# Where sixteen output-matrix products and the weights behind them stand among eight attention heads

## The chip, the core and the metric

The kernel runs on one core of a Trainium2 chip. The metric is the device time of one execution in microseconds (us), lower is better. Of the kernel before there are three timed runs: 1076.58, 1077.21 and 1078.67 us, median 1077.21.

The engines of the core are named as in the profile: PE is the matrix engine (TensorE), with PEld for its weight loads; DVE is VectorE, ACT is ScalarE, POOL is GpSimd, and SP issues most of the DMA transfers. Each has a queue of its own and works it off in order; semaphores make one engine wait for another. A line such as L853 is line 853 of the kernel.

## What is computed

One decoder block in float32 on a sequence of 1024 tokens with 1024 features. Eight heads of a softmax attention with a forgetting term and a gated branch ("spatial gating") share an input projection. Their results are put side by side and multiplied by one output matrix:

```python
xn = rmsnorm(h, norm_mix_g)
proj = xn @ w_in
att = forgetting_attention(q, k, v, log_f)            # 8 heads of 64
sg = chunked_spatial_gating(u, vg, gain, w_s, b_s)    # 512 wide
mix = concatenate([att, sg], axis=-1)
h = h + mix @ w_out                                   # (1024, 1024)
h = h + conv_ffn(rmsnorm(h), w_up, conv_w, conv_b, w_down)
return rmsnorm(h)
```

In `forgetting_attention` the logits are `q k^T / 8 + c_i - c_j` for j <= i, where c is a running sum of log-sigmoids. The change concerns `mix @ w_out`, which splits by rows of `w_out`: rows 512 to 1023 meet `sg` (the gated branch), rows 0 to 511 meet `att`.

## The kernel before, in words

**Precision.** A float32 operand is split into a rounded high part and the remainder (low part). One product is then three passes on PE: high by high, high by low, low by high. `split_w` (L150) makes the two parts: a cast on ACT or POOL gives the high part, a subtraction on DVE or POOL the low part.

**Stages.** In order of time: the input projection (to about 200 us), the spatial gating, the attention heads (about 216 to 395 us), the output matrix's attention half with the second norm (to about 445 us), the up projection with convolution, and the down projection. The last two are long runs of 128x512 products.

**An attention head** (`att_head`, L752). Five transfers of SP load the head's queries, keys and forgetting sums into two tiles (`x1`, `x2`, two buffers each, L754 to L760); so the loads of head h+2 start when head h has made its logits. The head goes through four steps i = 0 to 3, each with two blocks of 128 queries. For a block, POOL masks the diagonal (`affine_select`, L776), PE makes the logits (L783, L784), DVE adds and takes the row minimum (L786) and ACT the exponential (L789). Then, by pairs of key blocks, PE transposes (L812), ACT casts the high part (L813), DVE subtracts for the low part (L814) and PE multiplies by V (L822). ACT and DVE bring the sums out of PSUM (L828, L829). `row_tail` (L724) turns the row sums around through DRAM, and `pair_end` (L738) scales a pair of heads and splits it; for the first three pairs that is POOL's work, at step 2 of heads 2, 4 and 6.

**The filler** (`sg_out`, L833). The gated branch's half of `mix @ w_out` is 2 halves of the columns by 8 blocks of 128 tokens: 16 products of 12 matmuls (L851 to L853). It is a generator. The list `FILLS` (L20) says how many products are pulled ahead of the transposes of each of the 32 steps. Before the first product of each half, the half's weights are loaded (`wos`, two transfers of 512 KB into buffers `raw`) and split into four tiles `whl` (ACT casts, POOL subtracts). For each product a block of x is loaded into `raw`, DVE adds the product to it (L854), and SP stores the sum to `hpd` (L855). `raw` and `whl` have four buffers each. The list before gives 1, 2, 1, 2 products to the steps of heads 0 and 1 and 1, 2, 1 to the first three of head 2; the second half's weights are loaded and split at the place of product 8, the second product of head 1's step 1.

**The attention's output weights** (`wo_load`, L862). Four blocks of `woa`, 512 KB each. Blocks 0 and 1 go into the four `whl` tiles as soon as the filler is through with them, blocks 2 and 3 into tiles `G`. All casts and subtractions are POOL's. Blocks 0 and 1 stand behind the masks of head 5, blocks 2 and 3 behind the last mask of head 7; the transfers stand behind those of head 4. The products that need them (`wmm`, L959) begin at the end of head 7.

**Order.** The code is written in the order of importance. A planner puts it into one queue an engine when the kernel is built, from modelled costs: the earliest in the code that is ready goes first. `after(tc, later, earlier)` (L59) binds only the order of two instructions in the plan. So one step's instructions can stand among those of the step before, and an edit can move others around it.

Of the kernel before, what the change touches and what calls it, by code (L numbers as in the profile page):

```python
# [9 lines left out]
F32R = mybir.dt.float32r  # L10
BF16 = mybir.dt.bfloat16
AF = mybir.ActivationFunctionType
ALU = mybir.AluOpType
AX = mybir.AxisListType
P = 128
# [1 line left out]
BIG = 3.0e38  # L17
NFF = 22
WARM = 11
FILLS = [1, 2] * 10 + [2] + [0] * 11  # L20
FCFG = ("b", 4, 4)


# [35 lines left out]
def after(tc, later, earlier):  # L59
    tc.add_manual_dep(later.ins, earlier.ins.name, mybir.DependencyInfo(  # L60
        mybir.DependencyClass.NoSync, mybir.DependencyReason.DATA), reason="order")
# [3 lines left out]
def block_kernel(ctx: ExitStack, tc: tile.TileContext, xT, xtok, wuv, wv, wqk, wf, cpk, bfv,  # L65
                 ggain, g2r, gfr, wsp, woa, wos, wup, wdn, out):
    nc = tc.nc
    act, dve, pool, pe, sp = Line(nc.scalar, tc), Line(nc.vector, tc), Line(nc.gpsimd, tc), nc.tensor, nc.sync
# [6 lines left out]
    drm = ctx.enter_context(tc.tile_pool(name="drm", bufs=1, space=bass.MemoryType.DRAM))  # L75
    FILL = FILLS
    FTAG, FB, BB = FCFG
# [4 lines left out]
    def nm(s):  # L82
        uid[0] += 1
        return f"{s}_{uid[0]}"
# [6 lines left out]
    def sb(tag, shape, dt=F32):  # L91
        return (raws if tag == "raw" else late if tag in LATE else early).tile(shape, dt, tag=tag, bufs=BUFS[tag], name=nm(tag))
# [4 lines left out]
    def fbank():  # L97
        return psa.tile([P, 512], F32, tag=FTAG, bufs=FB, name=nm("pf"))
# [4 lines left out]
    def f32(ap):  # L103
        return ap.bitcast(F32)
# [45 lines left out]
    def split_w(src, hl, hi_eng="act", lo_eng="dve"):  # L150
        h, l = hl
        if hi_eng == "act":
            act.copy(h, src)  # L153
        elif hi_eng == "pool":
            pool.tensor_copy(h, src)
        else:
            dve.tensor_copy(h, src)
        eng = dve if lo_eng == "dve" else pool
        return eng.tensor_tensor(out=l, in0=src, in1=f32(h), op=ALU.subtract)  # L159
# [81 lines left out]
    def tsplit(src, neg=False, gate="keys"):  # L241
        w = ring()
        if neg:
            act.activation(w[:, 0], src, AF.Copy, scale=-1.0)
            behind(dve.scalar_tensor_tensor(out=w[:, 1], in0=src, scalar=-1.0, in1=f32(w[:, 0]),
                                            op0=ALU.mult, op1=ALU.subtract), gate)
        else:
            split_w(src, (w[:, 0], w[:, 1]))
        return w
# [85 lines left out]
    for j in range(2):  # L335
        t1, t2, t3 = tmp[j]
        for c in range(2):
            k = 2 * j + c
# [27 lines left out]
    for j in range(2):  # L366
        t2 = tmp[j][1]
        for c in range(2):
            k = 2 * j + c
# [35 lines left out]
    class Weights:  # L405
# [9 lines left out]
        def split(self, *names):  # L415
            for n in names:
                self.w[n] = tsplit(self.src[n])
# [223 lines left out]
    for hf in (1, 0):  # L641
        for c in range(4):
            src = vgt[hf][:, :, c * P:(c + 1) * P].rearrange("p t (g d) -> p g t d", g=2)
# [75 lines left out]
    loads = [None] * 8  # L719
    exs = []  # L720
    rows = [None] * 8
    sels = [[] for _ in range(8)]
# [29 lines left out]
    def att_head(h, order=(0, 1, 2, 3)):  # L752
# [13 lines left out]
        for i in order:  # L766
# [25 lines left out]
            if h == 7 and i == 3:  # L792
                wo_load((2, 3))
                row_tail(7, None)
# [36 lines left out]
            pair_end(3, None)  # L831

    def sg_out():  # L833
        for hf in range(2):
            o = slice(hf * 512, hf * 512 + 512)
            whs = []
            for kp in range(2):
                wr = sb("raw", [P, 2, 512])
                sp.dma_start(out=wr, in_=wos[hf, kp])
                for j in range(2):  # L840
                    w = sb("whl", [P, 2, 512], F32R)
                    split_w(wr[:, j, :], (w[:, 0], w[:, 1]), "act", "pool")
                    whs.append(w)
            for tt in range(8):
                ts_ = slice(tt * P, (tt + 1) * P)
                hs = sb("raw", [P, 512])
                sp.dma_start(out=hs, in_=xtok[ts_, o])
                ps = fbank()
                for k in range(4):
                    w = whs[k]  # L850
                    pe.matmul(ps, sgT[k][:, 0, ts_], w[:, 0, :], start=(k == 0), stop=False)  # L851
                    pe.matmul(ps, sgT[k][:, 0, ts_], w[:, 1, :], start=False, stop=False)  # L852
                    pe.matmul(ps, sgT[k][:, 1, ts_], w[:, 0, :], start=False, stop=(k == 3))  # L853
                dve.tensor_tensor(out=hs, in0=ps, in1=hs, op=ALU.add)  # L854
                sp.dma_start(out=hpd[tt, :, o], in_=hs)  # L855
                yield

    filler = sg_out()

    wo = []  # L860

    def wo_load(ks):  # L862
        for k in ks:
            wr = sb("raw", [P, 1024])
            after(tc, sp.dma_start(out=wr, in_=woa[k]), loads[4])
            if k < 2:
                w = [sb("whl", [P, 2, 512], F32R) for _ in range(2)]
            else:
                t = sb("G", [P, 2, 1024], F32R)
                w = [t[:, :, hf * 512:hf * 512 + 512] for hf in range(2)]  # L870
            for hf in range(2):
                src = wr[:, hf * 512:hf * 512 + 512]
                after(tc, pool.tensor_copy(w[hf][:, 0], src), sels[5][2 * k + hf] if k < 2 else sels[7][3])
                pool.tensor_tensor(out=w[hf][:, 1], in0=src, in1=f32(w[hf][:, 0]), op=ALU.subtract)
            wo.append(w)

    for h in range(8):
        if h == 7:
            for _ in filler:
                pass  # L880
            wo_load((0, 1))
        att_head(h)
# [569 lines left out]
```

## Time and profile before

| what | us |
|---|---|
| median of three runs | 1077.21 |
| the profiled execution, whole | 1076.71 |
| its span, first to last instruction | 1075.0 |
| PE busy in the span | 1062.7 |
| DVE busy | 892.4 |
| ACT busy | 568.0 |
| POOL busy | 249.5 |
| filler's products on PE, first to last start | 225.0 to 304.3 |
| second half's weights: ACT casts and POOL subtractions | 260.8 to 266.5 |
| first exponential of heads 0 to 7 | 227.0, 254.9, 287.7, 311.5, 324.9, 340.4, 356.6, 370.7 |

The profile is that of one execution; its whole time is 1.7 us over its span and 0.5 us under the median. A matmul's end is modelled, so PE's busy time says little on how full PE is. What counts is when the next matmul starts. The granted clock of PE was 0.998 of full speed over the span.

### The profile page before, as it was taken

Reading aid. Unit: us, or ns where it says so; the run is one execution under the profiler, and the core shown is the slowest. Engines: PE = TensorE matmul, PEld = TensorE weight load, DVE = VectorE, ACT = ScalarE, POOL = GpSimd, SP = SyncE. Lnnn points to the kernel's source line nnn. Section 1 sums busy time; section 2 is a strip of 40 time slices with the busy share of each in tenths; the row PEclk is TensorE's granted clock in tenths of the full one; section 3 lists DMA queues with packets and bytes.
Section 4 is the critical chain, followed back from the end, with each engine's and each line's share of the span. In section 5 each row is a group of like instructions: output and inputs, shape, how many; then the busy total and the mean of one; then the engine's idle time right before and its main releaser. Section 6 shows DMA issues by size and latency. Waiting matters only on the chain.

```text
span 1075.0 us, 14470 instructions
## 1 busy us (share of the span) xinstructions
PE 1062.7 (99%) x5013; PEld 876.6 (82%) x5013; DVE 892.4 (83%) x1363; ACT 568.0 (53%) x984; POOL 249.5 (23%) x223
## 2 busy tenths in 40 slices
PE   9999999999999999999999999999999999999997
PEld 7888788787888888878888888888888888888886
DVE  5985798775689969999899999989988776898774
ACT  6666644554468855764444444444444444454653
POOL 0002134233046541054333333333322000000000
PEclk9999999999999999999999999999999999999999
DMA  9242267937557445132244513222331899433442
GB/s 345 90 140 96 74 156 218 278 118 224 188 166 207 129 137 185 72 117 98 98 137 164 170 69 127 98 98 98 108 118 45 289 326 317 125 95 97 141 125 96
DMA packets 66297, 160.80 MB, mean 150 GB/s; under 512 B 7976, under 2 KB 8240, under 8 KB 66224
## 3 DMA queue, kind: packets, MB, share of 16 engines
q1 hardware_dynamic: 65792, 159.32, 45.4%
q8 instruction: 39, 0.64, 0.2%
q10 hardware_dynamic: 432, 0.57, 0.1%
q14 instruction: 34, 0.28, 0.1%
HBM read 117.06 MB, written 42.80 MB: 149 GB/s over the span
## 4 chain that ended last, share of the span: by engine, by line
PE 77%; ACT 2%; DVE 2%; issue 1%; POOL 0%; DMA 0%; DVEq 0%; ACTq 0%
PE k L1306 19%; PE qa L1054 11%; PE qc L1054 11%; PE qd L1054 11%; PE qb L1054 5%; PE pb L822 3%; PE pb L812 2%; PE ps L257 2%; PE pf L852 1%; PE pf L853 1%; PE pf L851 1%; PE ps L783 1%; PE ps L784 1%; PE pb L964 1%; PE pb L963 1%; PE pb L965 1%
## 5 line engine op out<-in xcount | busy, mean ns | idle before, releaser
L1306 PE MATMUL k<-whb,wha 128*128 128x512 f32 x924 | 209.7, 389 | 0.0
L1306 PEld LDWEIGHTS k<-whb,wha 128*128 128x128 f32 x924 | 173.3, 188 | 36.2 <-DVE wha L159 0.2
L1054 PE MATMUL qc<-xT,whb 128*128 128x512 f32 x540 | 129.8, 389 | 0.0
L1054 PE MATMUL qa<-xB,wha 128*128 128x512 f32 x528 | 127.2, 390 | 0.0
L1054 PEld LDWEIGHTS qc<-xT,whb 128*128 128x128 f32 x540 | 101.3, 188 | 21.2 <-ACT whb L153 0.2
L1054 PEld LDWEIGHTS qa<-xB,wha 128*128 128x128 f32 x528 | 98.8, 188 | 20.8 <-DVE wha L159 0.4
L153 ACT CAST wha<-sg 128x512 fp32r<-128x512 f32 x77 | 47.8, 622 | 96.9 <-PE k L1306 85.8
L153 ACT CAST whb<-sg 128x512 fp32r<-128x512 f32 x82 | 50.5, 617 | 86.6 <-PE qc L1054 67.0
L159 DVE TENSOR_TENSOR wha<-sg,wha 128x512 fp32r<-128x512 f32 x77 | 52.7, 687 | 41.1 <-ACT wha L153 41.0
L1054 PE MATMUL qd<-xB,whb 128*128 128x512 f32 x264 | 63.9, 389 | 0.5 <-DVE h L1173 0.5
L1054 PE MATMUL qd<-xT,whb 128*128 128x512 f32 x264 | 63.6, 389 | 0.0
L159 DVE TENSOR_TENSOR whb<-sg,whb 128x512 fp32r<-128x512 f32 x82 | 58.2, 710 | 4.4 <-ACT whb L153 4.3
L941 POOL TENSOR_TENSOR sg<-raw 128x512 f32<-128x512 f32 x20 | 30.7, 1535 | 134.0 <-DVE whb L159 75.7
L813 ACT CAST pt<-pb 128x512 fp32r<-128x512 f32 (+1 forms) x80 | 40.6, 543 | 38.5 <-PE pb L812 37.4
L1054 PE MATMUL qb<-xT,whb 128*128 128x512 f32 x252 | 60.9, 389 | 0.0
L822 PE MATMUL pb<-pt,V 128*128 128x256 f32 (+1 forms) x320 | 58.7, 298 | 1.6 <-ACT pt L813 1.2
L1054 PEld LDWEIGHTS qd<-xB,whb 128*128 128x128 f32 x264 | 49.5, 188 | 11.2 <-issue 0.9
L1054 PEld LDWEIGHTS qd<-xT,whb 128*128 128x128 f32 x264 | 49.6, 188 | 10.3
L822 PEld LDWEIGHTS pb<-pt,V 128*128 128x128 f32 x320 | 46.8, 188 | 13.5 <-ACT pt L813 8.9
L1054 PEld LDWEIGHTS qb<-xT,whb 128*128 128x128 f32 x252 | 47.3, 188 | 9.8
L814 DVE TENSOR_TENSOR pt<-pb,pt 128x512 fp32r<-128x512 f32 (+1 forms) x80 | 48.1, 632 | 8.0 <-ACT pt L813 7.4
L944 POOL TENSOR_TENSOR sg<-sg,raw 128x512 f32<-128x512 f32 x20 | 33.3, 1666 | 64.6 <-DVE whb L159 64.6
(399 smaller groups left out, 2306.9 us busy)
## 6 DMA issues: line engine op xcount, KB each, us to landing
raw<-wup SPq DMA_DIRECT2D x44, 512.0 KB, 3.5
sg<-hx SPq DMA_DIRECT2D x77, 256.0 KB, 2.8
hx<-hs SPq DMA_DIRECT2D x44, 256.0 KB, 3.7
hx<-ca SPq DMA_DIRECT2D x35, 256.0 KB, 2.0
xT<-wdn SPq DMA_DIRECT2D x28, 256.0 KB, 4.1
raw<-wqk SPq DMA_DIRECT2D x8, 512.0 KB, 4.7
qd<-G SPq DMA_DIRECT2D x16, 256.0 KB, 3.9
kd<-G SPq DMA_DIRECT2D x16, 256.0 KB, 3.3
```

What stands on the lines that cost most here:

```text
L153: act.copy(h, src)
L159: return eng.tensor_tensor(out=l, in0=src, in1=f32(h), op=ALU.subtract)
L257: pe.matmul(banks[m], xs(n, xi, k)[:, ms], w[:, wi, :], start=(first and k == 0 and c == 0), stop=(k == 3 and c == 2), skip_group_check=True)
L783: pe.matmul(ps[:, 0:e - c], A[:, qs], B[:, c:e], start=True, stop=False)
L812: pe.transpose(ptr[:, c:c + P], tj[jj][:, k * P:(k + 1) * P], ident)
L813: act.copy(pt[:, 0, 0:w], ptr[:, 0:w])
L814: dve.tensor_tensor(out=pt[:, 1, 0:w], in0=ptr[:, 0:w], in1=f32(pt[:, 0, 0:w]), op=ALU.subtract)
L822: pe.matmul(po[:, oo:oo + n], lhs, pt[:, s, o:o + n], start=(k == 0 and s == 0), stop=(s == 1 and half))
L941: pool.tensor_tensor(out=s[0], in0=a21, in1=a22, op=ALU.add)
L944: pool.tensor_tensor(out=s[3], in0=s[1], in1=a12, op=ALU.add)
L1054: pe.matmul(ps, w[:, wi, ks], xb[:, xi, k, :], start=(first and n == 0), stop=(n == 11), skip_group_check=True)
L1306: pe.matmul(banks[bk + m], xh[:, xi, ms], wh[:, wi, :], start=(first and p_ == 0 and n == 0), stop=(p_ == NP - 1 and n == 2), skip_group_c ...
```

## The change

The sixteen products are pulled at steps 0, 1 and 2 of heads 0, 1, 3 and 4 and at steps 0 and 1 of heads 2 and 5: the first half of the columns in heads 0 to 2, the second half in heads 3 to 5. The transfers of the second half's weights are issued at product 6 (head 2, step 0). Their split stands behind product 7 (head 2, step 1), with the subtractions on DVE; before it was at product 8 with the subtractions on POOL. The first half's split stays as it was.

The transfers of the attention's output weights stand behind those of head 6. For blocks 0 and 1, ACT makes the four casts, each behind an exponential of head 6 (its second, fourth, sixth and eighth), and POOL keeps the subtractions, each behind a mask of head 6. Blocks 2 and 3 keep their casts and subtractions on POOL at the end of head 7.

```diff
-FILLS = [1, 2] * 10 + [2] + [0] * 11
+FILLS = [1, 1, 1, 0, 1, 1, 1, 0, 1, 1, 0, 0, 1, 1, 1, 0, 1, 1, 1, 0, 1, 1] + [0] * 10
...
     def sg_out():
-        for hf in range(2):
-            o = slice(hf * 512, hf * 512 + 512)
-            whs = []
+        def load(hf):
+            wrs = []
             for kp in range(2):
                 wr = sb("raw", [P, 2, 512])
                 sp.dma_start(out=wr, in_=wos[hf, kp])
-                for j in range(2):
-                    w = sb("whl", [P, 2, 512], F32R)
-                    split_w(wr[:, j, :], (w[:, 0], w[:, 1]), "act", "pool")
-                    whs.append(w)
+                wrs += [wr[:, 0, :], wr[:, 1, :]]
+            return wrs
+
+        def split(wrs, lo_eng):
+            whs = []
+            for wr in wrs:
+                w = sb("whl", [P, 2, 512], F32R)
+                split_w(wr, (w[:, 0], w[:, 1]), "act", lo_eng)
+                whs.append(w)
+            return whs
+
+        whs = split(load(0), "pool")
+        for hf in range(2):
+            o = slice(hf * 512, hf * 512 + 512)
             for tt in range(8):
+                if hf == 0 and tt == 6:
+                    nxt = load(1)
                 ts_ = slice(tt * P, (tt + 1) * P)
...
                 sp.dma_start(out=hpd[tt, :, o], in_=hs)
+                if hf == 0 and tt == 7:
+                    whs = split(nxt, "dve")
                 yield
...
     def wo_load(ks):
         for k in ks:
             wr = sb("raw", [P, 1024])
-            after(tc, sp.dma_start(out=wr, in_=woa[k]), loads[4])
+            after(tc, sp.dma_start(out=wr, in_=woa[k]), loads[6])
...
             for hf in range(2):
                 src = wr[:, hf * 512:hf * 512 + 512]
-                after(tc, pool.tensor_copy(w[hf][:, 0], src), sels[5][2 * k + hf] if k < 2 else sels[7][3])
-                pool.tensor_tensor(out=w[hf][:, 1], in0=src, in1=f32(w[hf][:, 0]), op=ALU.subtract)
+                if k < 2:
+                    s = 2 * k + hf
+                    after(tc, act.copy(w[hf][:, 0], src), exs[49 + 2 * s])
+                    after(tc, pool.tensor_tensor(out=w[hf][:, 1], in0=src, in1=f32(w[hf][:, 0]), op=ALU.subtract),
+                          sels[6][s])
+                else:
+                    after(tc, pool.tensor_copy(w[hf][:, 0], src), sels[7][3])
+                    pool.tensor_tensor(out=w[hf][:, 1], in0=src, in1=f32(w[hf][:, 0]), op=ALU.subtract)
```

## The prediction, made before the result was known

> **What bounds the kernel now.** I read the page first.
>
> ```profile
> span 1075.0 us, 14470 instructions
> PE 1062.7 (99%) x5013; PEld 876.6 (82%) x5013; DVE 892.4 (83%) x1363; ACT 568.0 (53%) x984; POOL 249.5 (23%) x223
> ```
>
> PE is the bound of the whole, but a busy time of 99% hides small stalls, since ends are modelled. The change touches only the attention heads, so next I cut them at each head's first exponential (the L789 row on a `gg` tile; head 6's is shown) and asked for the engines' busy time in each stretch. Columns: stretch, its length, then PE, PEld, DVE, ACT, POOL. Heads 2 to 6:
>
> ```profile
> 356.57 0.39 ACT L789 ACTIVATE gg<-gg,mn 128x128 f32<-128x128 f32 x1
> ...
> 287.65:311.50 23.85, 23.85 (x134) 19.71 (x133) 15.65 (x41) 11.12 (x26) 7.80 (x10) 1.00 0.33 105
> 311.50:324.90 13.40, 13.29 (x92) 11.57 (x91) 12.99 (x38) 12.30 (x32) 3.33 (x8) 1.00 0.88 269
> 324.90:340.40 15.50, 14.89 (x105) 13.15 (x105) 14.03 (x36) 12.69 (x30) 7.67 (x10) 1.00 0.78 231
> 340.40:356.57 16.17, 15.48 (x112) 13.82 (x110) 14.67 (x41) 12.66 (x30) 12.30 (x21) 1.00 0.49 149
> 356.57:370.65 14.08, 13.80 (x99) 12.16 (x97) 13.49 (x40) 12.69 (x33) 4.93 (x9) 1.00 0.59 180
> ```
>
> Head 2 has four filler products beside it; DVE is busy 66% of it. Heads 3 to 6 have none: DVE is busy 97, 91, 91 and 96%, ACT 92, 82, 78 and 90%. So without the filler three engines run neck and neck, each waiting for the others' small steps.
>
> How much PE loses I count from starts. A filler matmul follows the last after (281.58 − 278.83)/12 = 0.229 us; a logit matmul of 512 columns after 0.23, of 384 after 0.17, narrower ones in proportion; a transpose after (1.20 − 0.27)/8, a product with V after (0.72 − 0.39)/3, both about 0.11:
>
> ```profile
> 278.83 0.39 PE L851 MATMUL pf<-whl,G 128*128 128x512 f32 x1
> ...
> 281.58 0.39 PE L851 MATMUL pf<-whl,G 128*128 128x512 f32 x1
> ```
> ```profile
> 339.29 0.34 PE L784 MATMUL ps<-x,x 128*128 128x384 f32 x1
> 339.46 0.39 PE L783 MATMUL ps<-x 128*128 128x512 f32 x1
> 339.69 0.40 PE L784 MATMUL ps<-x,x 128*128 128x512 f32 x1
> ```
> ```profile
> 356.72 1.20 PE L812 MATMUL pb<-ident,H 128*128 128x128 f32 x9
> ...
> 359.72 0.72 PE L822 MATMUL pb<-pt,V 128*128 128x256 f32 x4
> ```
>
> A head's 24 logit matmuls average 0.172 (12 wide, 4 of each narrower width), so its work at full pace is 24 × 0.172 + 76 × 0.11 = 12.5 us. The same stretches for PE alone, by tile: first logits (`ps`), then transposes and V (`pb`), then filler (`pf`); the first row of each is a stretch with filler, the others heads 3, 4 with 5, and 6.
>
> ```profile
> 267.14:304.50 37.36, 8.51 (x32) 1.00 0.48 156
> 311.50:324.90 13.40, 6.04 (x25) 1.00 0.88 269
> 324.90:356.57 31.67, 12.86 (x50) 1.00 0.63 189
> 356.57:370.65 14.08, 6.25 (x28) 1.00 0.59 180
> ```
> ```profile
> 267.14:304.50 37.36, 14.39 (x92) 1.00 0.48 156
> 311.50:324.90 13.40, 9.69 (x67) 1.00 0.88 269
> 324.90:356.57 31.67, 24.17 (x165) 1.00 0.63 189
> 356.57:370.65 14.08, 10.68 (x71) 1.00 0.59 180
> ```
> ```profile
> 267.14:304.50 37.36, 20.80 (x85) 1.00 0.48 156
> ```
>
> With filler: 32 × 0.172 + 92 × 0.11 = 15.6 us of attention and 85 × 0.229 = 19.5 of filler in 37.36, a stall of 2.3 us, or **0.145 us for each us of attention work**. Head 3: 11.7 of 13.40, 1.7 us, 0.148. Heads 4 and 5: 26.8 of 31.67, 4.9 us, **0.184**. Head 6: 12.6 of 14.08, 1.45 us, 0.115. This is the finding that keeps my forecast small: the filler hardly lowers PE's stall for a unit of attention; most of it seems to come with the heads' chains whether filler stands beside them or not. Only heads 4 and 5 stall clearly more.
>
> One more stall is plain in order of time, at the second half's split:
>
> ```profile
> 262.96 0.39 PE L851 MATMUL pf<-whl,G 128*128 128x512 f32 x1
> ...
> 265.33 0.50 PE L852 MATMUL pf<-whl,G 128*128 128x512 f32 x1 [0.28 <-POOL whl L159]
> ...
> 267.14 0.27 PE L812 MATMUL pb<-ident,wy 128*128 128x128 f32 x1
> ```
> ```profile
> 262.04 1.79 ACT L153 CAST whl<-raw 128x512 fp32r<-128x512 f32 x3
> ```
> ```profile
> 261.48 5.03 POOL L159 TENSOR_TENSOR whl<-raw,whl 128x512 fp32r<-128x512 f32 x4 [5.70 <-ACT whl L153]
> ```
>
> Product 8 runs from 262.96 to 267.14, 4.18 us where twelve matmuls need 2.75: PE waits 1.43 us for POOL's four subtractions (5.03 us).
>
> **The change part by part**, against the profiled execution's 1076.71 us (1.7 over its span, 0.5 under the median).
>
> *The split two products early: −1.43, +0.1.* The next product comes two steps later, in head 3, so the wait goes. New on ACT and DVE in head 2 are four casts (0.6 each) and, on DVE for POOL, four subtractions of 0.69:
>
> ```profile
> 394.49 0.69 DVE L750 TENSOR_TENSOR G<-H,G 128x512 fp32r<-128x512 f32 x1 [0.69 <-ACT G L749]
> ```
>
> Each `whl` tile is free once product 7 has used it, so the casts follow that product tile by tile, and its own 2.75 us hide most of them. If that cover fails, the transposes' casts behind them are late by up to 2.4 us. I take 0.1, near the covered end, as ACT and DVE both have idle time in head 2. Both transfers have a step's time more to land.
>
> *Eight products from heads 0 to 2 into heads 3 to 5: −1.04.* The work is the same; only stalls can go. At the filler stretch's 0.145, heads 4 and 5 lose 26.8 × 0.039 = 1.04 us less, head 3 nothing. Bounds: the filler, at three products (8.2 us) a head, could cover all stalls of heads 3 to 5 (−6.6); or heads 0 to 2, thinned out, could go to 0.184 (3 × 12.5 × 0.039 = +1.5). I take −1.04, the nearest row. What is late next is PE itself: 12.5 + 8.2 = 20.7 us a head against DVE's about 13 + 2. SP carries eight loads and eight stores more among the loads of heads 5 to 7. In head 1, with filler, the five loads of a head took 8.7 us to issue:
>
> ```profile
> 277.51 0.33 SPq L756 DMA_DIRECT2D x<-qd  x1
> ...
> 286.18 0.45 SPq L760 DMA_DIRECT2D x<-kd  x1
> ```
>
> They are wanted a head later, over 20 us with filler, so this costs nothing.
>
> *Attention's output weights in head 6: +0.3.* What moves is now in head 5 for block 1:
>
> ```profile
> 345.77 1.17 POOL L873 CAST whl<-raw 128x512 fp32r<-128x512 f32 x2
> 346.90 2.52 POOL L874 TENSOR_TENSOR whl<-raw,whl 128x512 fp32r<-128x512 f32 x2
> ```
>
> and the same for block 0 in head 4. POOL gets 4 × 0.6 us less in all, but 4 × 1.27 us of subtractions later. ACT gets 4 × 0.6 = 2.4 us in head 6, where it has 14.08 − 12.69 = 1.4 us idle; the rest, 1.0, can slip into head 7, where PE already fills time with `wmm`. Bounds 0 and +2.4; I take 0.3, nearer to the idle time's row. The four transfers pass the loads of heads 5 and 6 on SP and leave head 3's stretch, where the DMA share was 0.88; they are wanted a head later, so 0.
>
> Sum: −1.43 + 0.1 − 1.04 + 0.3 = −2.07 us. 1076.71 becomes 1074.6; from the median, 1077.21 becomes **1075.1**.
>
> **The rivals.**
>
> *More cover than I count.* Three products a head, spread over its steps, give PE something to do at each wait; if half the stalls of heads 3 to 5 (6.6 us) go, the sum is −1.43 − 3.3 = −4.7: **1072.5**. For: DVE at 91 to 97% there, and 66% in head 2. Against: 0.145 in the filler stretch.
>
> *Nothing.* The filler changes no stall and ACT's 1.0 in head 6 is paid: −0.4, **1076.8**. Head 3 (0.148 without filler) speaks for it.
>
> *Slower: POOL's chain at the end becomes the bound.* From head 6's end POOL has no pause:
>
> ```profile
> 368.48 2.54 POOL L744 TENSOR_TENSOR H<-H 128x512 f32<-128x512 f32 x2 [5.90 <-DMA H<-rsd]
> ...
> 374.58 0.61 POOL L776 TENSOR_SCALAR_AFFINE_SELECT H<-x 128x512 f32<-128x512 f32 x1
> ...
> 376.28 2.53 POOL L874 TENSOR_TENSOR G<-raw,G 128x512 fp32r<-128x512 f32 x2
> ```
> ```profile
> 382.00 0.39 PE L963 MATMUL ps<-G,G 128*128 128x512 f32 x1
> ```
>
> `pair_end`, head 7's last mask, then block 2, ready at 378.8 and used at 382.0. A subtraction that waits for ACT's cast holds all of that up. If the four (5.1 us) fall behind 368.5, block 2 is ready at 383.9, and PE waits 1.9 us; it decides from 3.2 us of delay. With ACT's 2.4 paid in full and no gain from the filler: −1.4 + 1.9 + 2.4 = +2.9, **1080.1**. For: ACT's casts wait for exponentials of head 6, the last of which end as `pair_end` begins. Against: three of the four can be done in POOL's pause before 368.5.
>
> *A locked port.* The trace shows four DVE subtractions with both inputs in SBUF taking 4.69 us beside POOL, where 4 × 0.69 = 2.8 would do:
>
> ```profile
> 395.87 4.69 DVE L159 TENSOR_TENSOR wha<-raw,wha 128x512 fp32r<-128x512 f32 x4 [0.69 <-ACT wha L153]
> ```
> ```profile
> 396.64 1.67 POOL L936 TENSOR_TENSOR raw<-raw,raw 128x512 f32<-128x512 f32 x1 [14.22 <-DVE wha L159]
> ```
>
> If head 2's four meet POOL's masks or `pair_end` so, they cost 1.9 us more, at worst all of it on the path: **1077.0**. The Trainium skill, page "SBUF — State Buffer", section "Who interferes with whom", says why: a DVE instruction with two SBUF inputs and a POOL instruction that reads SBUF share a read port, and the second to start waits for the whole of the first. By that rule the move to DVE is no plain gain; the trace agrees as far as these rows go. DVE's idle third in head 2 speaks against a cost.
>
> **How the numbers follow.** The forecast (1073.3 to 1076.8) has 0.42, more cover 0.21, nothing 0.10, slower 0.22, the port 0.05. A measurement of this kernel can tell about 0.2%, 2.15 us, from no change: under 1075.06 is faster, over 1079.36 slower. Half of the forecast's chance lies under that line: faster 0.21 + 0.21 = 0.42, same 0.21 + 0.10 + 0.05 = 0.36, slower 0.22. The range goes from 1071.8, a little under the case of more cover, to 1080.0; I leave out about 0.07 below and 0.11 above.
>
> **What would show it.** Right: no wait of PE on `whl` in head 3, product 8 within 2.8 us; stalls of 0.145 a us in heads 4 and 5; ACT's casts of `whl` within heads 6 and 7 and no longer head 6 than 14.5 us; block 2 ready before its first product. Wrong, upwards: PE waiting for ACT's cast `pt` or for `G` in heads 6 and 7. Wrong, downwards: heads 3 to 5 with hardly any stall. An order of the queues that the planner builds otherwise than the code suggests would upset all of it.

## The result and the profile after

The changed kernel takes 1083.80 us in the median of six runs (1082.67 to 1085.29), the kernel before 1077.17 in six runs beside it (1076.58 to 1078.67). The ratio is 1.0061, 95% interval 1.0048 to 1.0074: **slower by 0.6%, 6.6 us**. The forecast was 1075.1, its range ended at 1080.0.

Of the changed kernel's profile, only the span tells something; the busy times hardly differ. The profiled execution is the slowest of the six (1085.29 us):

```profile
span 1083.6 us, 14469 instructions
...
PE 1066.3 (98%) x5013; PEld 878.7 (81%) x5013; DVE 897.4 (83%) x1367; ACT 571.4 (53%) x988; POOL 245.2 (23%) x215
```

The span is 8.6 us longer (1083.6 − 1075.0), and all of it comes before the up projection: its first product starts at 446.0 us where it started at 437.4. What did PE wait for there? In head 2, from 279 to 293 us, and at the end of attention, from 379 to 395 us, three rows have nearly all of it. Columns: who waited, on whom, us in all, times, longest.

```profile
PE pb L822 <- DVE pt L814: 2.9, 1, 2.9
```
```profile
PE ps L983 <- POOL G L893: 1.9, 1, 1.9
PE ps L982 <- POOL G L892: 0.4, 1, 0.4
```

That is 5.2 us. Before, PE waits for no more than 0.4 us at a time in the heads. The other 3.4 us are seen only in the column of PE's granted clock (the third from the end in a view by stretches: stretch, length, busy times of PE, PEld, DVE, ACT, POOL, then clock, DMA share, GB/s). The changed kernel:

```profile
280.00:285.00 5.00, 2.77 (x20) 2.17 (x18) 4.80 (x5) 2.74 (x6) 4.54 (x4) 1.00 0.52 139
285.00:290.00 5.00, 4.35 (x22) 4.04 (x23) 3.55 (x9) 1.48 (x4) 4.58 (x7) 0.66 0.90 303
...
385.00:390.00 5.00, 3.03 (x13) 2.68 (x14) 0.38 (x3) 2.46 (x5) 5.00 (x6) 0.79 0.51 185
390.00:395.00 5.00, 5.00 (x33) 4.38 (x32) 1.82 (x3) 1.41 (x4) 0.99 (x1) 0.87 0.52 174
```

The kernel before in the same places:

```profile
285.00:290.00 5.00, 5.00 (x34) 4.49 (x34) 3.13 (x8) 3.03 (x8) 1.68 (x4) 1.00 0.76 211
...
385.00:390.00 5.00, 5.00 (x40) 4.36 (x39) 2.36 (x5) 3.19 (x6) 0.00 (x0) 1.00 0.37 111
```

Behind each stall PE runs for some 3.4 us at half its clock: about 5 × 0.34 = 1.7 us lost, and 5 × (0.21 + 0.13) = 1.7. Two stalls and two such stretches make 5.2 + 3.4 = 8.6 us, the difference of the two profiles (the medians differ by 6.6). Whatever else the change won or lost about cancels.

**The first stall** in order of time. DVE's four subtractions (L159) and POOL's `pair_end` of heads 0 and 1 (L744, L747) run at the same time, and DVE's own subtraction for the head (L814), which PE needs, stands behind them:

```profile
278.83 0.69 DVE L159 TENSOR_TENSOR whl<-raw,whl 128x512 fp32r<-128x512 f32 x1 [0.17 <-ACT whl L153]
...
280.46 2.97 POOL L744 TENSOR_TENSOR H<-H 128x512 f32<-128x512 f32 x2 [4.09 <-DVE whl L159]
280.81 4.18 DVE L159 TENSOR_TENSOR whl<-raw,whl 128x512 fp32r<-128x512 f32 x3
...
283.38 2.09 POOL L747 CAST A<-H 128x512 fp32r<-128x512 f32 x2
284.91 1.74 DVE L814 TENSOR_TENSOR pt<-pb,pt 128x512 fp32r<-128x512 f32 x3
...
285.65 0.58 PE L822 MATMUL pb<-pt,V 128*128 128x256 f32 x1 [2.88 <-DVE pt L814]
```

Three subtractions of 0.69 take 4.18 us, and POOL's two casts, 1.17 before, take 2.09: both engines slow each other.

**The second stall** begins on SP. Its queue stands from 360 to 370.78 before a load of the gated product's weights into `raw` (L933): that buffer holds block 0 of attention's output weights until POOL has made its subtractions. Behind it stands head 5's row tail (L735), though ACT had sent its data off at 364.07. `pair_end` waits for it and starts at 376.44, where before it started at 368.48. For the last 2.8 of these 8 us POOL stands and waits for the row tail; up to then, 373.66, it works off masks and three of the moved subtractions (L889). The fourth subtraction and block 2 (L893) come behind `pair_end`, and PE waits for block 2:

```profile
358.56 1.54 SPq L760 DMA_DIRECT2D x<-kd  x1
370.78 0.34 SPq L933 DMA_DIRECT2D raw<-wup  x1
371.22 0.44 SPq L735 DMA_DIRECT2D H<-rsd  x1
```
```profile
368.21 2.54 POOL L889 TENSOR_TENSOR whl<-raw,whl 128x512 fp32r<-128x512 f32 x2
...
370.98 1.28 POOL L889 TENSOR_TENSOR whl<-raw,whl 128x512 fp32r<-128x512 f32 x1
...
376.44 2.56 POOL L744 TENSOR_TENSOR H<-H 128x512 f32<-128x512 f32 x2 [2.78 <-DMA H<-rsd]
...
382.56 1.29 POOL L889 TENSOR_TENSOR whl<-raw,whl 128x512 fp32r<-128x512 f32 x1
...
384.92 2.50 POOL L893 TENSOR_TENSOR G<-raw,G 128x512 fp32r<-128x512 f32 x2
```
```profile
387.47 0.50 PE L983 MATMUL ps<-G,G 128*128 128x512 f32 x1 [1.95 <-POOL G L893]
```

Theory, then: the stall beside `pair_end`, SP's order, and half clock behind both, against a small gain by the spreading. Rivals: the spreading itself is the loss; the burst of casts and subtractions stalls PE wherever it stands; POOL's subtractions are late by themselves; the half clock has another cause. Eighteen experiments follow, two of them on the same kernel. Ratios are to the kernel before, whose median lay between 1077.3 and 1077.6 in the five groups.

### The profile page after: what moved, and what is told of

Read it like the earlier page. It is cut to its first block, busy times and chain, and to the rows that moved or that the text cites. A ratio compares the mean times of both kernels' runs of the same rounds, so it can differ in the third digit from the quotient of the medians.

```text
span 1083.6 us, 14469 instructions
## 1 busy us (share of the span) xinstructions
PE 1066.3 (98%) x5013; PEld 878.7 (81%) x5013; DVE 897.4 (83%) x1367; ACT 571.4 (53%) x988; POOL 245.2 (23%) x215
## 4 chain that ended last, share of the span: by engine, by line
PE 74%; DMA 3%; DVE 2%; POOL 1%; issue 1%; ACT 1%; SPq 0%; POOLq 0%; ACTq 0%; DVEq 0%
PE k L1325 19%; PE qa L1073 11%; PE qc L1073 11%; PE qd L1073 11%; PE qb L1073 5%; PE pb L822 3%; PE ps L257 2%; PE pb L812 2%; PE pf L862 1%; PE pf L864 1%; PE pf L863 1%; PE pb L983 1%; PE pb L982 1%; PE pb L984 1%; PE ps L783 1%
## 5 line engine op out<-in xcount | busy, mean ns | idle before, releaser
L1325 PE MATMUL k<-whb,wha 128*128 128x512 f32 x924 | 209.8, 389 | 0.0
L159 DVE TENSOR_TENSOR wha<-sg,wha 128x512 fp32r<-128x512 f32 x77 | 53.1, 691 | 40.9 <-ACT wha L153 40.7
L159 DVE TENSOR_TENSOR whb<-sg,whb 128x512 fp32r<-128x512 f32 x82 | 58.4, 712 | 4.7 <-ACT whb L153 4.6
L814 DVE TENSOR_TENSOR pt<-pb,pt 128x512 fp32r<-128x512 f32 (+1 forms) x80 | 47.8, 633 | 10.2 <-ACT pt L813 10.0
```

Source lines behind the costliest of these rows:

```text
L814: dve.tensor_tensor(out=pt[:, 1, 0:w], in0=ptr[:, 0:w], in1=f32(pt[:, 0, 0:w]), op=ALU.subtract)
L1325: pe.matmul(banks[bk + m], xh[:, xi, ms], wh[:, wi, :], start=(first and p_ == 0 and n == 0), stop=(p_ == NP - 1 and n == 2), skip_group_c ...
```

## The experiments

**One part alone.** *Fills:* the new `FILLS`, nothing else.

```diff
-FILLS = [1, 2] * 10 + [2] + [0] * 11
+FILLS = [1, 1, 1, 0, 1, 1, 1, 0, 1, 1, 0, 0, 1, 1, 1, 0, 1, 1, 1, 0, 1, 1] + [0] * 10
```

> The kernel before with the new list of fills alone: the products of the gated branch's output matrix are spread to head 5, the second split of its weights stays where it was in the text (at the ninth product, now in head 2), loaded there and with its low parts on GpSimd. My theory puts the loss of the changed kernel (+6.6 us) down to two collisions, the VectorE split beside the pair's end in head 2 (about +4.5) and the SyncE queue held in heads 6 and 7 (about +5), and takes the spreading itself for a gain of about 3: expected 1074 to 1076 us. A rival, that the spreading itself is the loss because later heads have too little VectorE and ScalarE time for it, expects 1079 us or more.

Measured: 1078.35 (1076.14 to 1083.67), ratio 1.0011 [0.9996, 1.0025]. Neither was right: no gain and no certain loss, and a spread of 7.5 us that the kernel before does not have.

*Split:* `sg_out` of the changed kernel with the old list.

> The kernel before with the new order of load and split alone: weights of the second half loaded two products ahead, the four low parts subtracted on VectorE after the eighth product, which with the old list of fills is in head 1, where no pair's end runs on GpSimd. My theory (the subtractions are slow only beside the casts and subtractions of a pair's end on GpSimd): the stall of about 4 us does not come, the old wait of 1.4 us goes, 1075.5 to 1077.5 us. The rival, that a burst of four subtractions on VectorE and four casts on ScalarE between two heads' steps costs its 4 us wherever it stands: 1080 us or more.

1076.55, ratio 0.9992 [0.9984, 1.0001]: as my theory said. The same four casts and subtractions stall nothing in head 1; the longest wait of PE there is:

```profile
PE pb L812 <- ACT H L789: 0.3, 1, 0.3
```

*Output weights:* `wo_load` of the changed kernel alone.

> The kernel before with the new treatment of attention's output weights alone (loaded behind head 6's loads, casts of the first two blocks on ScalarE in head 6, subtractions on GpSimd from head 6's selects on). My theory: GpSimd frees the first block's buffer only at about 370 us, SyncE's load into that buffer waits for it and holds the row tail of head 5 behind it, the pair's end of heads 4 and 5 comes 7 to 8 us later and with it the low parts of the last two blocks: 1081 to 1083 us, and the trace shows GpSimd's pair's end at about 375 us or later. The rival, that this only bites together with the fills that now reach head 5, expects 1077 us and a pair's end at about 368 us.

1079.86, ratio 1.0021 [1.0012, 1.0030]: a loss of 2.5 us, less than the theory said and not by its way. Here the planner puts the row tail ahead of the load, and `pair_end` starts at 367.69, as the rival said. What is late is a mask of head 7 that DVE needs, behind `pair_end` and two subtractions on POOL. PE stands 1.1 us for that; the rest of the loss is not explained:

```profile
DVE H L786 <- POOL H L776: 1.7, 1, 1.7
```

*Fills and split,* with the output weights as before.

> The changed kernel with attention's output weights treated as before: the new list of fills and the new split together, without the third part. My theory: the stall of 2.9 us beside the pair's end in head 2 is there, and the half clock behind it (3.4 or 6.8 us at 0.50, so 1.7 or 3.4 us lost); the stall of heads 6 and 7 is not: 1079 to 1081.5 us. As fills alone gave 1078.35 and the split alone 1076.55, the two together would then cost 2 us more than apart. The rival, that the third part makes no difference once the fills reach head 5: 1083 us or more.

1081.16, ratio 1.0037 [1.0023, 1.0050]. Fills alone +1.0 (0.0 when it was run again, below), split alone −0.8, both +3.5: **the two parts collide**. With the +2.5 of the third part that is +6.0, near the whole change's +6.6. In this profile `pair_end` came later, only one subtraction met it (1.76 us), and the stall was 1.7 us.

**The first stall.** *Low parts on POOL:*

```diff
-    whs = split(nxt, "dve")
+    whs = split(nxt, "pool")
```

> The changed kernel with the low parts of the second split on GpSimd in place of VectorE, all else as changed. My theory: VectorE no longer runs beside GpSimd's pair's end, the 4 to 5 us that TensorE loses between 280 and 290 us shrink to 1 to 2: 1079.5 to 1081.5 us. The rival, that the loss there is the burst itself (casts on ScalarE ahead of the head's own copies) or that GpSimd's selects are then late instead: 1083 to 1085 us as before the edit.

1078.41, ratio 1.0015 [1.0003, 1.0027]: 5.4 us under the changed kernel, more than expected. DVE is free; but POOL's queue now holds back head 3's masks, and PE waits 1.8 us at 292. The planner's order at the end differs too, and the second stall is not in this profile, so not all of the 5.4 belongs to the first.

*Split one step earlier:*

```diff
-FILLS = [1, 1, 1, 0, 1, 1, 1, 0, 1, 1, 0, 0, ...
+FILLS = [1, 1, 1, 0, 1, 1, 1, 1, 1, 0, 0, 0, ...
```

> The changed kernel with the list of fills changed in two places, so that the eighth product and with it the second split come one step earlier (head 2's first step in place of its second), ahead of the pair's end on GpSimd. My theory: VectorE's four subtractions then take 0.69 us each, the stall of 2.9 us at 282.8 and the 3.5 us of half clock behind it go: 1078.5 to 1080 us, with the loss of heads 6 and 7 still there. The rival, that the burst of casts and subtractions stalls TensorE wherever it stands: 1082.5 us or more, with the stall about 5 us earlier.

1080.60, ratio 1.0035 [1.0021, 1.0048]: 3.2 less than the changed kernel. Clear of `pair_end` the last three subtractions take 1.88 us in place of 4.18, but PE still waits:

```profile
277.31 1.88 DVE L159 TENSOR_TENSOR whl<-raw,whl 128x512 fp32r<-128x512 f32 x3
```
```profile
PE pb L822 <- DVE pt L814: 1.4, 1, 1.4
```

So the shared time with POOL is about half of the stall in head 2, and the burst itself, without a product queued behind it on PE, the other half. Theory and rival each had a part. PE's wait for `G` is shorter here, too (1.1 us), and this profile has no half clock in the heads, so not all of the 3.2 us belongs to the first stall.

**SP's order.**

```diff
-        sp.dma_start(out=attF[p]...[row tail])
+        tails[h] = sp.dma_start(out=attF[p]...[row tail])
...
-            after(tc, d, loads[7])
+            after(tc, d, tails[5 + i])
```

> The changed kernel with one order on SyncE turned round: the first two loads of the gated product's weights wait for the row tails of heads 5 and 6, which stood behind them. What the trace of the changed kernel shows at the end of attention: SyncE stands before the first of these loads until 370.78 us, so the row tail of head 5 is issued at 371.22 and the pair's end on GpSimd starts at 376.44; TensorE then stands about 2 us at 385, and its granted clock is 0.50 for 3.5 us behind that. My theory: with the order turned round both go, 1078.5 to 1080.5 us, and the profiled run shows one stretch of half clock (about 285 to 289 us) in place of two. The rival, that GpSimd's subtractions in heads 6 and 7 are late by themselves: 1082.5 us or more.

1080.96, ratio 1.0036 [1.0024, 1.0048]: 2.8 less. `pair_end` starts at 373.71 without a wait, and PE's wait for `G` and the second half clock are gone. It is still 5.2 us later than in the kernel before, as POOL is busy with masks and three of the moved subtractions up to then; so much the rival had right. Head 2 shows what kept the gain from being more: the same stall of 2.9 us, and this time the half clock lasts twice as long, 2 × 5 × (0.35 + 0.33) = 6.8 us. PE works for 5.75 of them, so 2.9 us are lost:

```profile
285.00:290.00 5.00, 2.40 (x11) 2.40 (x12) 4.55 (x9) 0.40 (x1) 5.00 (x6) 0.65 0.80 256
290.00:295.00 5.00, 5.00 (x28) 4.67 (x27) 3.95 (x10) 3.05 (x8) 1.54 (x4) 0.67 0.97 287
```

*Both edits:*

> Both edits together: second split one step earlier, and SyncE's order turned round. If the two stalls and the two stretches of half clock are the whole of the loss, and the spreading is worth about 2 us as the stretch from 300 to 360 us says: 1074 to 1076 us, at or below the kernel before. If a third loss is in the change (ScalarE's casts in head 6, or the spreading): 1077.5 us or more.

1079.26, ratio 1.0012 [1.0003, 1.0020]. Of the 6.6 us, 1.6 are left (1079.26 against 1077.64), as the second case said. The longest stall in this profile is the 1.5 us that the burst still costs PE in head 2.

**What a stall costs.** In the kernel before, useless subtractions ahead of one block of the down product, where nothing else is changed (n = 12 and 16):

```diff
             split_w(src, (wh[:, 0], wh[:, 1]))
+            for _ in range(n if (xn_, p_) == ('A11', 5) else 0):
+                dve.tensor_tensor(out=wh[:, 1], in0=src, in1=f32(wh[:, 0]), op=ALU.subtract)
```

> The kernel before with twelve useless subtractions of 0.69 us on VectorE (8.3 us) ahead of one weight block of the down product's first product: the same values are written again, and TensorE waits once, by what is left of the 8.3 us when its buffers ahead are used up (an estimate: 0 to 3 us). Theory: a stall under about 2 us costs its own length; from about 2 us on TensorE's granted clock falls to 0.50 for 3.4 or 6.9 us behind it in most runs, 1.7 or 3.4 us more. The rival, that the half clock in the traces has another cause than the stall: the stall's own length alone, and no run under a mean clock of 0.998.

> The same with sixteen subtractions, 2.8 us more of stall than with twelve. Theory: stall over 2.5 us, so half clock in every run: 1077.6 + stall + 1.7 or 3.4 us, two groups of times at mean clocks of 0.997 and 0.996 or 0.995. Rival: 2.8 us more than with twelve and clocks as of the kernel before.

1087.96 and 1092.17, ratios 1.0099 [1.0086, 1.0112] and 1.0133 [1.0120, 1.0146]. The stalls were longer than estimated, 8.39 and 11.70 us. With twelve, PE's row and the stretches from 875 us on:

```profile
881.74 5.62 PE L1308 MATMUL k<-whb,wha 128*128 128x512 f32 x15 [8.39 <-DVE whb L1302]
```
```profile
875.00:880.00 5.00, 0.00 (x0) 0.00 (x0) 5.00 (x10) 0.00 (x0) 0.00 (x0) 0.56 0.86 280
880.00:885.00 5.00, 3.26 (x8) 2.58 (x9) 1.69 (x3) 0.00 (x0) 0.00 (x0) 0.50 1.02 389
885.00:890.00 5.00, 5.00 (x22) 4.06 (x21) 2.05 (x4) 2.28 (x4) 0.00 (x0) 0.91 0.79 299
```

From PE's return at 881.74 the clock is 0.50 until 885 and a little beyond: 3.26 × 0.50 + 5 × 0.09 = 2.1 us. 8.39 + 2.1 = 10.5, measured 10.4. With sixteen:

```profile
885.64 1.65 PE L1308 MATMUL k<-whb,wha 128*128 128x512 f32 x3 [11.70 <-DVE whb L1302]
```
```profile
885.00:890.00 5.00, 4.36 (x10) 3.47 (x11) 0.59 (x1) 0.54 (x2) 0.00 (x0) 0.50 1.01 406
890.00:895.00 5.00, 5.00 (x21) 4.01 (x20) 2.54 (x4) 1.75 (x4) 0.00 (x0) 0.89 0.54 193
```

11.70 + 4.36 × 0.50 + 5 × 0.11 = 14.4, measured 14.6. **The half clock is the stall's own doing**: it is there where a stall was put and nothing else changed.

The traces show when it comes. Half clock lasts 3.41, 6.83, 10.24 or 13.65 us in the kernels run here, one to four times 3.41 us, and within a trace its starts lie whole steps of that length apart (285.47 and 387.87 in the changed kernel: 102.40 = 30 × 3.413). Cut along these steps, the changed kernel reads as follows (stretch, length, PE's busy time, clock, DMA share, GB/s):

```profile
282.05:285.47 3.42, 0.71 (x6) 1.00 0.79 231
285.47:288.88 3.41, 3.23 (x15) 0.50 0.94 309
384.45:387.87 3.42, 1.09 (x4) 1.00 0.45 153
387.87:391.28 3.41, 3.41 (x18) 0.50 0.44 154
```

PE stands for 2.7 and 2.3 us of the step ahead of each drop. The smallest such idle time with a drop behind it is 1.8 us, in the run with SP's order turned round; the largest without one is 1.6 us, in the run with POOL's low parts:

```profile
283.11:286.52 3.41, 1.59 (x11) 1.00 0.58 177
```
```profile
292.75:296.16 3.41, 1.77 (x14) 1.00 1.02 360
```

All twenty traces agree: from the first full clock to the last product, half clock follows each step with 1.8 us of idle PE or more, and it follows no step at full clock with 1.6 us or less (nothing lies between). So it matters how a stall falls on the steps: one of 1.95 us that lay in one step with 0.4 us of waiting ahead of it brought half clock, one of 1.8 us that two steps shared did not. The Trainium skill, page "TensorE: Matmul & The Clock Gate", Part 1, says that PE's clock drops to half after an idle window of about 3.4 us that runs freely. The halving and the length of the window agree here; that the whole window must be idle does not, as 1.8 us of 3.41 were enough.

*Fills once more:*

> The fills alone once more, for the spread of its runs and a second profile. Theory: a stall of 3.0 us at 292 us in every run, and half clock of 3.4 us behind it in about half of them, so that a profile without half clock shows the same stall and a span shorter by 1.7 us or more; times in two groups again. Rival: the two groups differ in the length of the stall.

1077.59 (1075.40 to 1081.20), ratio 0.9997 [0.9986, 1.0007]. Of the 24 runs of this kernel, the seven at a mean clock of 0.996 or 0.997 took 1079.1 to 1083.7, sixteen of the seventeen at 0.998 or 0.999 at most 1078.6. But the rival is right as well: the stall's length varies. First and second profile of the same kernel, POOL's split, DVE's wait for a mask behind it, and PE:

```profile
288.39 4.99 POOL L159 TENSOR_TENSOR whl<-raw,whl 128x512 fp32r<-128x512 f32 x4
...
293.66 0.35 DVE L786 CUSTOM_DVE_ANT_0 H<-ps,H,mn 128x128 f32<-128x128 f32 x1 [3.58 <-POOL H L776]
...
294.67 1.11 PE L822 MATMUL pb<-pt,V 128*128 128x256 f32 x4 [3.00 <-DVE pt L814]
```
```profile
290.04 4.95 POOL L159 TENSOR_TENSOR whl<-raw,whl 128x512 fp32r<-128x512 f32 x4
...
295.28 0.35 DVE L786 CUSTOM_DVE_ANT_0 H<-ps,H,mn 128x128 f32<-128x128 f32 x1 [5.50 <-POOL H L776]
...
296.29 1.01 PE L822 MATMUL pb<-pt,V 128*128 128x256 f32 x3 [4.92 <-DVE pt L814]
```

In the second, head 1's row tail was issued 1.8 us later (279.74 against 277.91), POOL's `pair_end` and split moved with it, and the stall grew by 1.9 us. Neither profile is of a run without half clock, so how the two share the spread stays open.

**Is the spreading worth anything?** Seven versions tried to have it without a stall. *Split one step earlier, output weights as before:*

> The changed kernel with the second split one step earlier and the treatment of attention's output weights as before (loads behind head 4's loads, casts and subtractions on GpSimd from head 5 on). My theory: neither stall, no casts on ScalarE in head 6: 1073.5 to 1075.5 us, the fastest so far. The rival, that the output weights on GpSimd collide with products that now reach head 5: 1077 us or more.

1080.21, ratio 1.0026 [1.0017, 1.0034]: missed. The stalls are 1.4 us at 278 and 1.2 at 376, where DVE waits 1.9 us for a mask behind `pair_end`.

*Two products queued behind the split,* `FILLS = [1, 1, 1, 0, 1, 1, 1, 1, 3, 0, 0, 0, 1, 1, 1, 0, 1, 1, 1, 0]`, with SP's order turned round; then with the output weights as before, without and with SP's new order:

> The changed kernel with SyncE's order turned round and the list of fills changed so that two products follow right behind the second split in the same step (three fills in head 2's first step, and the last two of the list gone). The split alone, with the old list, had a product queued behind it on TensorE and stalled it nowhere over 0.92 us; in the runs with the split one step earlier nothing was queued behind it, and TensorE stood 1.4 to 1.5 us. My theory: a burst of casts and subtractions costs little where TensorE has products queued behind it: no stall over 1 us in head 2, so no half clock in any run, times within 1.5 us of each other, 1075.5 to 1077.5 us. The rival, that the burst costs its VectorE and ScalarE time anyway: 1078.5 us or more.

> The same covered split, with attention's output weights as before and SyncE's order as it falls. The run with the split one step earlier and the old output weights gave 1080.2 us, of which a stall of 1.4 us at 278 and one of 1.2 us at 376 us can be seen; here the first should go: 1076.5 to 1078.5 us. The rival (burst costs anyway): 1080 us.

> As the run before, and the first loads of the gated product's weights put behind the row tails of heads 5 and 6 on SyncE, so that GpSimd's pair's end of heads 4 and 5 does not wait for them. If that wait makes head 7's selects late, which VectorE needs: 1074.5 to 1076.5 us, faster than the kernel before. If not, the same as without the new order.

1078.59 (1.0007 [0.9998, 1.0016]), 1079.44 (1.0022 [1.0010, 1.0034]), 1079.43 (1.0014 [1.0005, 1.0023]). Head 2 has no stall in any of them: a cover helps. But a stall came up elsewhere. With the old output weights two of their loads hold SP up to 342.91 (rows of the last of the three). The first waits 5.4 us for a `raw` buffer whose product, now later, is still being stored; the second waits 5.1 us for POOL's subtractions of block 0, which stand behind `pair_end` and masks. Head 6's loads go out behind them, and PE waits for those at 351 us, with half clock behind it:

```profile
337.09 5.82 SPq L878 DMA_DIRECT2D raw<-woa  x2
...
345.97 0.60 SPq L760 DMA_DIRECT2D x<-kd  x1
```
```profile
PE ps L784 <- DMA x<-kd: 2.9, 1, 2.9
```

*Milder list:* `FILLS = [1, 1, 1, 1, 1, 1, 1, 3, 1, 1, 0, 1, 1, 1, 1, 0]`, new split, old output weights.

> The kernel before with the new split and a milder list: one product in each step, three in the step of the second split (head 1's last, two of them queued behind it), none beside the pair's end of heads 0 and 1, the last product in head 3; attention's output weights as before. Theory: the spreading is worth 1.3 us for every 20 us in which it puts one product into each step, if no stall comes with it: 1075 to 1076.5 us, no gap over 1 us, clocks of 0.998 and 0.999. Rival: the spreading gives nothing, its gain in heads 3 is a loss in heads 0 to 2, where two products a step stood: 1076.5 to 1078 us.

1078.91, ratio 1.0010 [1.0002, 1.0019]; a stall of 1.5 us at 346, again DVE behind a mask behind `pair_end`.

*`pair_end` called later* in the covered version with SP's order turned round. Then the same in the milder list, with SP's order turned round and the changed kernel's output weights moved to head 5 (`loads[5]`, `exs[41 + 2 * s]`, `sels[5][s]`):

```diff
-            if h in (2, 4, 6) and i == 2:
-                pair_end(p - 1, sel)
+            if (h, i) in {(2, 2), (5, 2), (7, 2)}:
+                pair_end((2, 5, 7).index(h), sel)
```

> The covered split with SyncE's order turned round (1078.6 us, one stall of 1.3 us at 377), and the pair's ends of heads 2 and 3 and of heads 4 and 5 called one head later, behind the select of the third step of heads 5 and 7. Theory: the stall at 377 goes, as VectorE's select no longer stands behind the pair's end: 1076 to 1077.7 us. Rival: the pair's end is then late for attention's output matrix itself and the stall comes there: 1078.5 us or more.

> The milder list with the covered split in head 1, attention's first two weight blocks cast on ScalarE and subtracted on GpSimd in head 5 in place of head 6, SyncE's order turned round, and the pair's ends called later as in the run before: none of the stalls found so far. Theory: spreading without a stall is worth 2 to 3 us: 1074 to 1076 us, faster than the kernel before, clocks of 0.998 and 0.999 throughout. Rival: the spreading is worth nothing, 1077 us or more though no stall over 1 us shows.

In the covered version before this edit, POOL's masks of head 7 (L776) stood behind `pair_end` and a subtraction, and DVE waited:

```profile
369.54 2.54 POOL L744 TENSOR_TENSOR H<-H 128x512 f32<-128x512 f32 x2 [1.27 <-DMA H<-rsd]
...
376.87 1.69 POOL L776 TENSOR_SCALAR_AFFINE_SELECT H<-x 128x128 f32<-128x128 f32 x4
```
```profile
DVE H L786 <- POOL H L776: 2.2, 1, 2.2
```

With the edit two masks go first:

```profile
368.01 0.39 POOL L776 TENSOR_SCALAR_AFFINE_SELECT H<-x 128x256 f32<-128x256 f32 x1
368.38 2.53 POOL L744 TENSOR_TENSOR H<-H 128x512 f32<-128x512 f32 x2
```

No wait of DVE on a mask is left there, and PE stands nowhere in the heads for over a us in either version. The times are 1078.31 (1.0007 [0.9998, 1.0017]) and 1078.05 (1.0005 [0.9997, 1.0014]): no gain that can be measured. Two of the twelve runs of the first still show a clock of 0.997, at 1080.7 and 1081.3 us, so some runs probably have a stall that the profile does not. **In the two versions without a stall in their profiles the spreading is worth about nothing**; my theory that it is worth 2 to 3 us fell. From the first exponential of head 0 to the first up product their profiles take 209.8 us (226.9 to 436.7) and 210.8; the kernel before takes 210.3 (210.4 and 210.5 in the two kernels with useless subtractions, whose heads are the same), and the new split with the old list 209.6. So what the better of the two gains there is no more than the split gains without any spreading. No version beats the kernel before by more than the measurement can tell; the new split with the old list is the nearest.

## Why the prediction was wrong

- **The new split, "+0.1": the step that failed.** It said that the casts follow the product tile by tile under its own 2.75 us and that ACT's and DVE's idle time in head 2 pays. The product ran from 276.76 to about 280, the subtractions from 278.83 to 285.0: no product was queued behind them on PE, and `pair_end` stood beside them. Measured: 2.9 us of stall and 1.7 of half clock, where +0.1 had been put down. An idle third of an engine says nothing about the place where its work lands.
- **The locked port, 0.05 at +1.9.** On DVE it cost 2.3 us (4.18 for the three subtractions beside POOL, 1.88 clear of it); the price was about right, the chance was not. The list of fills was at hand: the split stands at head 2's step 1, `pair_end` is called at step 2. The rule of the Trainium skill that the prediction cites (page "SBUF — State Buffer", section "Who interferes with whom") agrees with these rows, and POOL is slowed as well, 2.09 for 1.17 in its casts.
- **The output weights, "+0.3".** ACT's casts were not the matter: PE's waits for ACT in the heads come to 0.4 us. The rival of POOL's chain had the place and part of the mechanism. Of the 8 us by which `pair_end` was late, POOL worked off masks and moved subtractions in the first 5.2; the last 2.8 are SP's queue, which the prediction did not go through past the loads of heads 5 to 7. That it had PE's wait to the tenth (1.9 us) is luck: it put block 2 at 383.9, and it was ready at 387.4, while PE came later as well. The part alone cost 2.5 us by another order of POOL's queue. Head 6, which was to take no more than 14.5 us, took 16.8 (first exponentials at 356.8 and 373.6).
- **The spreading, −1.04.** The two versions without a stall show −0.5 and +0.5 in the stretch of the heads (209.8 and 210.8 against 210.3), and against the split alone (209.6) no gain at all. The term was put too high, though its bounds, −6.6 to +1.5, hold. That the filler hardly lowers PE's stall for a unit of attention was the right reading. The wait at the old split went: no wait of PE on `whl` is left from 290 to 357 us.
- **What no step had: the clock.** Each stall was priced at its length. 3.4 of the 8.6 us between the two profiles are half clock behind stalls of 2.9 and 1.9 us.
- **The planner.** The last sentence of the prediction named it as what would upset all; it did. SP's order in the changed kernel is not that of either part alone.

## What to carry to other kernels

Price a moved burst by what is queued behind it on the bound engine and by what runs beside it at that place, not by idle shares of its engines; and price a stall of two us or more of a matrix engine that was full at more than its length. When an edit shifts work among queues that run in order, go through the order of each queue (here SP's and POOL's) from the edit to the end of the stage: a load that waits for a buffer holds everything behind it. A gap-free version is the test of whether the wanted gain exists at all.

## What the runs showed of the hardware

- PE's granted clock falls to 0.50 at the next mark of a grid of 3.41 us steps, if PE stood for 1.8 us or more of the step before it; 1.6 us did not do it. That was 1.8 to 4.4 us after PE had stopped (in the changed kernel stalls from 282.77 and 385.52, half clock from 285.47 and 387.87). The half clock cost 1.5 to 3.1 us of full pace once PE worked again.
- DVE subtractions with both inputs in SBUF and POOL's casts or subtractions beside them slow each other: 1.09 to 1.75 us for 0.69 on DVE, 1.07 for 0.6 for a cast on POOL.
- Some kernels with a stall spread over 5.8 to 7.5 us from run to run (the fills alone, the low parts on POOL, the split one step earlier), where the kernel before mostly stays within about 3. Others do not: the changed kernel spreads over 2.6, the two with useless subtractions over 2.2 and 0.8.
